# A two-layer macaron block in float32r: where the tiles of x and h begin in the SBUF

## The chip, the cores and the metric

The kernel runs on one core of one Trainium2 chip. Its time is the device time in microseconds (us) of one execution, and lower is better. Three executions of the kernel before were timed; their median is what a version is judged by.

## The reference

The input is x of 512 tokens by 1024 features, in float32. Two layers follow one another, each in the same frame:

```
mod = silu(c) @ ada_w[i] + ada_b[i]          # 9 vectors of 1024: shift, scale, gate, three times
h = rms_norm(x) * (1 + sc1) + sh1;  x += 0.5 * g1 * swiglu(h, wg1, wu1, wd1)   # hidden 2816
h = rms_norm(x) * (1 + sc2) + sh2;  x += g2 * mix(h)
h = rms_norm(x) * (1 + sc3) + sh3;  x += 0.5 * g3 * swiglu(h, wg2, wu2, wd2)
x = rms_norm(x)
```

In layer 0 `mix` is differential attention (8 heads, two softmaxes of 64-wide queries and keys per head, values 128 wide, a bias by distance, causal). In layer 1 it is a spatial gating unit: gelu(h @ w_in) split into u and v, v normed and mixed over each 128 tokens by a lower-triangular matrix per group, times u, times w_out. Nearly all arithmetic is in the products with the weights: gate, up and down of four feed-forward blocks, and the projections of the two mixers.

## The kernel before

Features lie on partitions. x is eight tiles x0 to x7 of 128 features by 512 tokens (2048 bytes on each partition). The normed input h is held in two parts, hh (h rounded to float32r) and hl (the rest), eight tiles each, of the same shape. A weight chunk arrives by DMA in a raw tile wr, and `Stream.conv` (line 183) splits it into wh and wl in the same manner: a cast on ACT, a subtraction on DVE. `Stream.get` keeps the loads some chunks ahead of the products. Every product is then three matmuls, `mm3` (line 582): wh with the high part of the activation, wh with the low part, wl with the high part. Each matmul has its own load of the stationary operand.

Four shapes of these products carry the kernel:

- Gate and up of the feed-forward blocks (`ffn`, line 702) and the u half of the gating unit: stationary is a 128x128 piece of wh or wl, moving is hh or hl with all 512 tokens. The rows call them mm<-hh,wh, mm<-hl,wh and mm<-hh,wl, moving operand first.
- Down (`down_g`, line 637): stationary is again a piece of wh or wl, moving is an activation pair from the pool `apool` (named a). The last half of a block's columns is done in two halves of 256 tokens, so that the next norm can begin.
- The first group of gate and up of the later feed-forward blocks goes by halves of 256 tokens too, moving hh and hl.
- `tm_block` (line 602), for q, k, v of the attention and the v half of the gating unit: stationary is a 128-token piece of hh or hl, moving is wh or wl with 256 columns (mm<-wh,hh, mm<-wh,hl, mm<-wl,hh).

The scheduler of the tile framework orders the instructions of each engine by priority and adds the waits; only at the start (lines 380 to 880, up to the end of `start_products`) are they issued as written. Pools take their room in the SBUF in the order in which they are opened (lines 78 to 84), one after the other, and tiles within a pool likewise, each rounded up to 32 bytes per partition. The first pool, `cst`, holds ident (512 bytes), mhalf (128), ones (4, so 32), ones_r (512), then the 24 tiles of x, hh and hl, then some thirty small vectors.

What this makes of the addresses can be worked out from the sizes: ident begins at 16512 bytes, which is 128 beyond a multiple of 512 (class 128). ones_r begins at 17184, class 288. x0 begins at 17696, class 288, and since each of the 24 tiles is 2048 bytes, all of x, hh and hl are of class 288. The small vectors behind them bring `cst` to 68928, class 320; there wrp begins, and all tiles of wrp, whp, apool, npool and accp and the large ones of the pools opened later (the feed-forward's, the attention's) are multiples of 512 bytes or follow such, so wr, wh, wl, a, acc, silu, qk, v and qkT are all of class 320. Class 288 is 32 beyond a multiple of 64; class 320 is a multiple of 64.

Of the kernel before, what the change touches and what calls it, by code (L numbers as in the profile page):

```python
# [11 lines left out]
F32 = mybir.dt.float32  # L12
# [7 lines left out]
P = 128  # L20
S = 512
# [15 lines left out]
def _bucket_runs():  # L37
    """Runs of equal bucket along y, where the distance is n = S - 1 - y."""
    n = np.arange(S - 1, -1, -1)
    nf = np.maximum(n, 1).astype(np.float32)  # L40
    large = MAX_EXACT + (
        np.log(nf / MAX_EXACT) / math.log(MAX_DIST / MAX_EXACT) * (BUCKETS - MAX_EXACT)
    ).astype(np.int32)
    b = np.where(n < MAX_EXACT, n, np.minimum(large, BUCKETS - 1))
    runs, lo = [], 0
    for y in range(1, S + 1):
        if y == S or b[y] != b[lo]:
            runs.append((lo, y, int(b[lo])))
            lo = y
    return runs  # L50


class InOrder:
    """An engine; while on, its instructions are issued in the order they are written."""

# [14 lines left out]
def macaron_kernel(ctx: ExitStack, tc: tile.TileContext, T: dict, out: bass.AP):  # L70
# [6 lines left out]

    cst = ctx.enter_context(tc.tile_pool(name="cst", bufs=1))
    wrp = ctx.enter_context(tc.tile_pool(name="wrp", bufs=4))
    whp = ctx.enter_context(tc.tile_pool(name="whp", bufs=5))  # L80
    apool = ctx.enter_context(tc.tile_pool(name="apool", bufs=24))
    npool = ctx.enter_context(tc.tile_pool(name="npool", bufs=2))
    tiny = ctx.enter_context(tc.tile_pool(name="tiny", bufs=4))
    accp = ctx.enter_context(tc.tile_pool(name="accp", bufs=1))
# [31 lines left out]
    def rsqrt(v, n):  # L116
        """v [P, n] positive and normal -> 1/sqrt(v): bit estimate, then Newton steps."""
        if n <= 4:
            y = tiny.tile([P, 32], F32, tag="rq_y", name=nm("rq_y"))
            G.tensor_tensor(out=y[:, :n], in0=v, in1=mhalf[:, :n], op=ALU.pow)  # L120
            return y[:, :n]
        i = tiny.tile([P, 32], U32, tag="rq_i", name=nm("rq_i"), bufs=2)
        j = tiny.tile([P, 32], I32, tag="rq_j", name=nm("rq_j"), bufs=2)
        ts(i[:, :n], v.bitcast(U32), 1, ALU.logical_shift_right)
        ts(j[:, :n], i[:, :n].bitcast(I32), -1.0, ALU.mult, 1597463007.0, ALU.add)
        y = j[:, :n].bitcast(F32)
        for it in range(3):
            t = tiny.tile([P, 32], F32, tag="rq_t", name=nm("rq_t"), bufs=2)
            tt(t[:, :n], y, y, ALU.mult)
            u = tiny.tile([P, 32], F32, tag="rq_u", name=nm("rq_u"), bufs=2)  # L130
            stt(u[:, :n], t[:, :n], -0.5, v, ALU.mult, ALU.mult)
            z = tiny.tile([P, 32], F32, tag="rq_y", name=nm("rq_y"))
            stt(z[:, :n], u[:, :n], 1.5, y, ALU.add, ALU.mult)
            y = z[:, :n]
        return y

    # ---------------------------------------------------------------- constants
    ident = cst.tile([P, P], F32, name="ident")
# [11 lines left out]

    x = [cst.tile([P, S], F32, name=f"x{d}") for d in range(KT)]
    h_hi = [cst.tile([P, S], F32R, name=f"hh{d}") for d in range(KT)]
    h_lo = [cst.tile([P, S], F32R, name=f"hl{d}") for d in range(KT)]

    ada_w, ada_b = T["ada_w"], T["ada_b"]

    # ------------------------------------------------------------- weight stream
    plan = []
# [53 lines left out]

    # ------------------------------------------------------- modulation vectors
    mod = {}
    acc_of = {}

    def finish_mod(l, m, ps):
        """ps [P, KT] holds c_act @ ada_w for this vector, one column per feature tile."""
        o = cst.tile([P, KT], F32, name=f"mod{l}_{m}")
# [30 lines left out]
    def flush_late(force=False):  # L250
        """The sums over partitions follow once the accumulation is surely through."""
        for it in list(late):
# [19 lines left out]

    # --------------------------------------------------------------------- plan
    ffn_w = {
# [6 lines left out]
    def groups_of(first):  # L281
        """FFN hidden tiles: two halves, each a list of groups of tiles."""
        if first:
            h1 = [[0, 1, 2]] + [[f, f + 1] for f in range(3, 11, 2)] + [[11]]
            h2 = [[f, f + 1] for f in range(12, 22, 2)]
        else:
            h1 = [[f, f + 1] for f in range(0, 12, 2)]
            h2 = [[f, f + 1] for f in range(12, 22, 2)]
        return h1, h2
# [8 lines left out]
    def get_k(key, nk):  # L298
        """The chunks of one block of columns, as they come: (k0, kn, hi, lo)."""
        for k0, kn in kchunks(nk):  # L300
# [77 lines left out]

    # ------------------------------------------------------------ start: loading
    in_order(True, V, A, PE, G, SY)  # L380
# [48 lines left out]
    def small_inputs():  # L429
        """Gains and biases of the rest, a column per tile of 128 features."""  # L430
        rows = a_tile()
# [27 lines left out]
    def attn_inputs():  # L459
        """The bias by distance for every head, and lambda."""  # L460
        # tab[h, y] = 8 * bias at distance S-1-y, masked beyond
        rb = a_tile()[:H, :BUCKETS]
# [9 lines left out]
        nc.gpsimd.dma_start(out=sc[:, S:], in_=tail[:H, : NCOL - S])  # L472
        # bias[h, p, c] = tab[h, 127 - p + c]: distance p + 384 - c
        par["bias"] = dram.tile([H, P, S], F32, name="bias")
# [11 lines left out]

    # ------------------------------------------------------------------- norms
    def bcast_tokens(r, tts, dst):
        """dst[:, 128*i ...] = r[token] on every partition."""
        for i, t in enumerate(tts):  # L490
# [8 lines left out]
    class Norm:  # L499
        """RMS norm over features (partitions and tiles) of x, by halves of the tokens."""  # L500

# [23 lines left out]
        def s1(self, hf):  # L525
# [9 lines left out]
            if self.pre is not None:  # L535
                # of the scaled x / sqrt(v): 1 / (sqrt(v) sqrt(m / v + EPS)) = 1 / sqrt(m + EPS v)
                m = tiny.tile([P, 2], F32, tag="nw", name=nm("nw"))
# [44 lines left out]
    def mm3(ps, w_hi, w_lo, a_hi, a_lo, first, last):  # L582
        """ps += w.T @ a with the operands split in two parts each."""
        PE.matmul(ps, lhsT=w_hi, rhs=a_hi, start=first, stop=False)
        PE.matmul(ps, lhsT=w_hi, rhs=a_lo, start=False, stop=False)
        PE.matmul(ps, lhsT=w_lo, rhs=a_hi, start=False, stop=last)

    # ------------------------------------------------------------------ phases
    def glu(pg, pu, fp):
# [5 lines left out]
    def split(v):  # L595
        """v = hi + lo, hi its rounding to float32r and lo the rest."""
        hi, lo = a_tile(F32R), a_tile(F32R)
# [13 lines left out]
    def token_major(key, done):  # L611
        """h (tokens) x one block of 256 columns; done(half, bank) takes two token tiles each."""
        W = list(get_k(key, KT))
# [8 lines left out]
    def token_major2(keys, dones):  # L622
        """Two blocks at once, the first half of the tokens ahead of the second."""
        Ws = [list(get_k(key, KT)) for key in keys]
# [12 lines left out]
    def down_g(tag, acts, gate, norm=None):  # L637
        """x += gate * (w.T @ acts); with norm, its sums and first half follow, the rest is pending."""
        na = len(acts)
# [112 lines left out]

    # --------------------------------------------------- start: x, norm, first mods
    sp2 = tiny.tile([P, 2, NB], F32, tag="ss0", name="sp2")
# [129 lines left out]

    # ------------------------------------------------------- differential attention
    with tc.tile_pool(name="attn", bufs=2) as at:
# [9 lines left out]
        def proj(p):  # L896
            """Generator: the products of a pair of heads, q and k normed and turned."""
            res = R[p] = {}
# [61 lines left out]
        def stage_a(n):  # L960
            """Logits, bias and softmax of one tile of queries of one head."""
            p, hh, i = steps[n]
# [30 lines left out]
        def stage_b(n):  # L993
            """The attention matrix turned, keys on partitions."""
            p, hh, i = steps[n]
# [8 lines left out]
        def stage_c(n):  # L1004
            """Times the values; after a head's (for the last one: half a head's) last tile its norm."""
            p, hh, i = steps[n]
# [24 lines left out]
        def stage_d(p, hh, t0, nt):  # L1031
            """A head's output turned, features on partitions."""
            o = oo.pop((p, hh, t0))
# [65 lines left out]

    # ------------------------------------------------------------- spatial gating  # L1100
    with tc.tile_pool(name="sgu", bufs=1) as sg:
# [73 lines left out]

    # -------------------------------------------------------------------- output
    oa = out.rearrange("o s d -> (o s) d")
# [50 lines left out]
```

## Time and profile before

| | us |
|---|---|
| three timed executions | 1961.03, 1957.12, 1956.90 (median 1957.12) |
| the profiled execution, first to last instruction (its span, the one time that the profile gives) | 1959.7 |
| TensorE (PE) busy in it | 1929.9 (98%) |
| VectorE (DVE) busy | 1081.5 (55%) |
| ScalarE (ACT) busy | 684.0 (35%) |
| GpSimd (POOL) busy | 69.8 (4%) |

PEld is TensorE's load of stationary operands, which runs beside PE. A matmul's row gives its own duration, some 0.4 us for 512 columns; successive ones overlap, so the time from one start to the next is shorter, and it is read from a stretch of the chain of waits: length over count. Nearly all instructions are issued by a helper, so their line is L63, and groups are told apart by tile names.

### The profile page before, as it was taken

What the parts mean: (1) busy time and instruction counts of PE and PEld (TensorE: products, weight loads), DVE (VectorE), ACT (ScalarE), POOL (GpSimd) and SP (SyncE); (2) the same over time, 40 slices, a digit from 0 to 9 for tenths busy, and PEclk for the clock granted to TensorE, in tenths of its full rate; (3) what the DMA queues carried; (4) which work ended last, traced back from release to release, by engine and by line L of the source; (5) the groups of instructions that cost most, each with busy time, mean ns of one, the idle gap of its engine ahead of it and who ended that gap; (6) DMA issues with size and microseconds to landing.
All of it is one profiled execution on the core that took longest, in us unless ns stands there. A gap on an engine that the chain in (4) does not pass through costs nothing.

```text
span 1959.7 us, 25722 instructions
## 1 busy us (share of the span) xinstructions
PE 1929.9 (98%) x10263; PEld 1635.1 (83%) x10263; DVE 1081.5 (55%) x1953; ACT 684.0 (35%) x1095; POOL 69.8 (4%) x81
## 2 busy tenths in 40 slices
PE   7999999999999999999999999999999999999998
PEld 6788888899997888888889888888898898888888
DVE  6856465576778854444457644444577763333332
ACT  5433123235555542222334232223252342222223
POOL 4300000000000000000000000000000000000000
PEclk8899999999999999999999999999999999999999
DMA  9666565532222254444443544443544333333321
GB/s 264 202 190 201 152 205 162 183 124 87 76 76 78 65 179 124 138 135 143 121 148 98 162 127 141 139 140 100 169 134 156 98 98 97 97 97 94 89 86 44
DMA packets 204109, 255.74 MB, mean 130 GB/s; under 512 B 9167, under 2 KB 177265, under 8 KB 203989
## 3 DMA queue, kind: packets, MB, share of 16 engines
q1 hardware_dynamic: 201552, 249.60, 41.6%
q0 software_dynamic: 2336, 4.46, 0.8%
q8 instruction: 80, 1.31, 0.3%
q14 instruction: 41, 0.33, 0.0%
q10 hardware_dynamic: 100, 0.04, 0.0%
HBM read 251.94 MB, written 4.21 MB: 131 GB/s over the span
## 4 chain that ended last, share of the span: by engine, by line
PE 93%; DVE 4%; ACT 1%; SPq 1%; DMA 1%; issue 0%; POOL 0%; POOLq 0%; ACTq 0%; DVEq 0%
PE mm L63 91%; PE sm L63 2%; DVE acc L63 2%; DVE a L63 1%; SPq L63 1%; DVE wl L63 0%; ACT a L63 0%; POOL rq_y L63 0%; DMA ada<-in_ada_w_dram 0%; ACT wh L63 0%; DVE x L63 0%; DVE hl L63 0%; DMA a<-in_x_dram 0%; ACT sq L63 0%; DVE A L63 0%
## 5 line engine op out<-in xcount | busy, mean ns | idle before, releaser
L63 DVE TENSOR_TENSOR wl<-wr,wh 128x1024 fp32r<-128x1024 f32 (+1 forms) x320 | 384.3, 1203 | 421.1 <-ACT wh L63 418.3
L63 PE MATMUL mm<-hh,wh 128*128 128x512 f32 (+1 forms) x1568 | 602.9, 385 | 8.3 <-ACT hh L63 8.3
L63 PE MATMUL mm<-hl,wh 128*128 128x512 f32 (+1 forms) x1568 | 602.4, 384 | 1.7 <-DVE hl L63 1.7
L63 PE MATMUL mm<-hh,wl 128*128 128x512 f32 (+1 forms) x1568 | 600.9, 384 | 0.0
L63 ACT CAST wh<-wr 128x1024 fp32r<-128x1024 f32 (+2 forms) x328 | 336.7, 1029 | 743.4 <-PE mm L63 680.9
L63 PE MATMUL mm<-a,wh 128*128 128x512 f32 (+1 forms) x2112 | 542.0, 346 | 0.0
L63 PEld LDWEIGHTS mm<-a,wh 128*128 128x128 f32 x2112 | 368.7, 190 | 50.9 <-DVE mx L63 1.3
L63 PE MATMUL mm<-a,wl 128*128 128x512 f32 (+1 forms) x1056 | 364.5, 345 | 2.2 <-DVE wl L63 2.2
L63 PEld LDWEIGHTS mm<-hh,wh 128*128 128x128 f32 x1568 | 296.9, 189 | 72.6 <-ACT hh L63 10.5
L63 PEld LDWEIGHTS mm<-hl,wh 128*128 128x128 f32 x1568 | 297.1, 189 | 65.8 <-DVE hl L63 3.6
L63 PEld LDWEIGHTS mm<-hh,wl 128*128 128x128 f32 x1568 | 296.6, 189 | 62.9 <-DVE wl L63 0.2
L63 DVE SCALAR_TENSOR_TENSOR acc<-wr,c_col,acc 128x1024 f32<-128x1024 f32 x112 | 143.7, 1283 | 185.8 <-DMA wr<-in_ada_w_dram 185.4
L63 PEld LDWEIGHTS mm<-a,wl 128*128 128x128 f32 x1056 | 200.8, 190 | 26.6 <-DVE wl L63 2.9
L63 PE MATMUL mm<-wh,hh 128*128 128x256 f32 x512 | 146.5, 287 | 0.0
L63 PE MATMUL mm<-wl,hh 128*128 128x256 f32 x512 | 142.9, 280 | 0.0
L63 PE MATMUL mm<-wh,hl 128*128 128x256 f32 x512 | 142.6, 280 | 0.0
L63 ACT CAST a<-silu 128x512 fp32r<-128x512 f32 x88 | 54.6, 621 | 152.1 <-DVE silu L63 152.1
L63 PEld LDWEIGHTS mm<-wh,hh 128*128 128x128 f32 x512 | 96.4, 188 | 8.6 <-issue 6.9
L63 DVE SCALAR_TENSOR_TENSOR x<-mm,mod,x 128x512 f32<-128x512 f32 (+1 forms) x116 | 70.7, 619 | 59.4 <-PE mm L63 58.9
L63 PEld LDWEIGHTS mm<-wl,hh 128*128 128x128 f32 x512 | 96.4, 188 | 0.0
L63 PEld LDWEIGHTS mm<-wh,hl 128*128 128x128 f32 x512 | 96.1, 188 | 0.1
L63 DVE TENSOR_TENSOR silu<-silu,mm 128x512 f32<-128x512 f32 x88 | 60.1, 686 | 44.0 <-PE mm L63 43.8
(166 smaller groups left out, 1149.6 us busy)
## 6 DMA issues: line engine op xcount, KB each, us to landing
wr<-in_ada_w_dram SPq DMA_DIRECT2D x128, 512.0 KB, 3.6
wr<-in_ffn_wg_dram SPq DMA_DIRECT2D x84, 512.0 KB, 3.9
wr<-in_ffn_wu_dram SPq DMA_DIRECT2D x84, 512.0 KB, 3.9
wr<-in_ffn_wd_dram SPq DMA_DIRECT2D x84, 512.0 KB, 3.5
wr<-in_attn_w_qkv_dram SPq DMA_DIRECT2D x24, 512.0 KB, 3.6
ada<-in_ada_w_dram SPq DMA_DIRECT2D x16, 512.0 KB, 6.0
wr<-in_sgu_w_in_dram SPq DMA_DIRECT2D x16, 512.0 KB, 3.8
wr<-in_attn_w_o_dram SPq DMA_DIRECT2D x8, 512.0 KB, 3.5
```

The source lines that it names most:

```text
L63: r = f(*a, **kw)
```

## The change

Two pools change places and one is new. `tiny`, the pool of small vectors (5632 bytes, eleven times 512), is opened second instead of sixth, and x, hh and hl move from `cst` into a pool of their own, `hxp`, opened third. `cst` then ends at 19776 (class 320), `tiny` at 25408 (class 320), and there x0 begins; the 24 tiles of x, hh and hl are of class 320 like all other large tiles. wrp begins at 74560 and whp, apool and npool move up with it by 5632 bytes, which leaves their class at 320; accp and what is opened later stays where it was. ident and ones_r stay at classes 128 and 288. No instruction is added or taken out, and none has another shape or operand. The diff also empties docstrings and comment lines, which issue nothing.

```
     cst = ctx.enter_context(tc.tile_pool(name="cst", bufs=1))
+    tiny = ctx.enter_context(tc.tile_pool(name="tiny", bufs=4))
+    hxp = ctx.enter_context(tc.tile_pool(name="hxp", bufs=1))
     wrp = ctx.enter_context(tc.tile_pool(name="wrp", bufs=4))
     whp = ctx.enter_context(tc.tile_pool(name="whp", bufs=5))
     apool = ctx.enter_context(tc.tile_pool(name="apool", bufs=24))
     npool = ctx.enter_context(tc.tile_pool(name="npool", bufs=2))
-    tiny = ctx.enter_context(tc.tile_pool(name="tiny", bufs=4))
     accp = ctx.enter_context(tc.tile_pool(name="accp", bufs=1))
...
-    x = [cst.tile([P, S], F32, name=f"x{d}") for d in range(KT)]
-    h_hi = [cst.tile([P, S], F32R, name=f"hh{d}") for d in range(KT)]
-    h_lo = [cst.tile([P, S], F32R, name=f"hl{d}") for d in range(KT)]
+    x = [hxp.tile([P, S], F32, name=f"x{d}") for d in range(KT)]
+    h_hi = [hxp.tile([P, S], F32R, name=f"hh{d}") for d in range(KT)]
+    h_lo = [hxp.tile([P, S], F32R, name=f"hl{d}") for d in range(KT)]
```

## Rows read from the trace of the kernel before

**Rows 1.** The page: busy time of the engines, and the granted clock in 40 slices.
```profile
PE 1929.9 (98%) x10263; PEld 1635.1 (83%) x10263; DVE 1081.5 (55%) x1953; ACT 684.0 (35%) x1095; POOL 69.8 (4%) x81
...
PEclk8899999999999999999999999999999999999999
```

**Rows 2.** Stretches of the run: length, busy time and count of PE, granted clock, DMA share, GB/s.
```profile
690.00:1040.00 350.00, 350.00 (x1639) 1.00 0.44 136
1480.00:1880.00 400.00, 399.56 (x1952) 1.00 0.33 101
```

**Rows 3.** The page, chain of waits: shares of the span by engine.
```profile
PE 93%; DVE 4%; ACT 1%; SPq 1%; DMA 1%; issue 0%; POOL 0%; POOLq 0%; ACTq 0%; DVEq 0%
```

**Rows 4.** PE's waits: releaser, us in total, times, longest us.
```profile
PE mm L63 <- ACT hh L63: 8.3, 5, 3.0
PE mm L63 <- DVE wl L63: 2.2, 3, 1.5
```

**Rows 5.** Groups of matmuls by shape: count, busy us, mean ns, idle before.
```profile
L63 PE MATMUL mm<-hh,wh 128*128 128x512 f32 x1376 | 549.1, 399 | 8.3 <-ACT hh L63 8.3
L63 PE MATMUL mm<-a,wh 128*128 128x512 f32 x1216 | 376.7, 391 | 0.0
L63 PE MATMUL mm<-a,wh 128*128 128x256 f32 x896 | 165.3, 286 | 0.0
L63 PE MATMUL mm<-wh,hh 128*128 128x256 f32 x512 | 146.5, 287 | 0.0
L63 PE MATMUL mm<-hh,wh 128*128 128x256 f32 x192 | 53.8, 283 | 0.0
```

**Rows 6.** Chain of waits in gate and up, moving hh and hl: start, length, count.
```profile
1079.93 80.27 PE mm L63 x344
```
**Rows 7.** Chain of waits in down, 512 columns, moving a.
```profile
1194.94 60.07 PE mm L63 x265
1714.88 50.32 PE mm L63 x222
```
**Rows 8.** Chain, 256 columns: moving a; moving wh, stationary hh; moving hh, stationary wh.
```profile
1920.00 16.44 PE mm L63 x137
...
1439.89 28.36 PE mm L63 x243
...
1588.00 12.07 PE mm L63 x102
```
**Rows 9.** Chain within down: four matmuls of 512 columns, moving a, stationary ones_r.
```profile
387.42 0.93 PE sm L63 x4
```
**Rows 10.** Chain within attention: eight transposes of 128 columns, each with its own load.
```profile
515.00 0.87 PE sm L63 x8
```
**Rows 11.** Groups on DVE and ACT that touch x or h, and their like on a.
```profile
L63 DVE SCALAR_TENSOR_TENSOR x<-mm,mod,x 128x512 f32<-128x512 f32 x60 | 44.3, 748 | 29.1 <-PE mm L63 28.9
L63 DVE SCALAR_TENSOR_TENSOR a<-a,rs,a 128x512 f32<-128x512 f32 x8 | 6.0, 750 | 0.2
L63 ACT ACTIVATE sq<-x 128x512 f32<-128x512 f32 x15 | 9.3, 628 | 10.9 <-DVE x L63 9.6 <-DVE ssq L63 1.1
L63 ACT ACTIVATE a<-a 128x512 f32<-128x512 f32 x15 | 9.4, 632 | 13.0 <-DVE a L63 11.2 <-DMA a<-in_x_dram 1.8
```
**Rows 12.** Chain at the start: one of six such pieces of DVE, and PE behind them.
```profile
52.85 4.59 DVE acc L63 x6
...
69.14 32.92 PE mm L63 x129
```
## The prediction

> **What bounds the kernel now.** I read four views, from coarse to fine. The page first: PE is busy for 98% of the span, no other engine for more than 55%, and the clock is granted in full in all but the first two of 40 slices [rows 1]. The stretches next: from 690 to 1040 us PE is busy for 350.00 of 350.00 us, from 1480 to 1880 for 399.56 of 400, with the DMA engines below a half [rows 2]. The chain of waits puts 93% of the span on PE [rows 3], and PE's own waits are a few us: the longest groups are 8.3 us for hh and 2.2 us for wl [rows 4]. So in the feed-forward blocks PE never runs dry, and what counts there is not who waits but how far apart the starts of successive matmuls are. For that I divide pieces of the chain by their counts.
>
> The reader should see that the same instruction has two paces. In gate and up, moving hh or hl, 344 matmuls take 80.27 us: 233.3 ns each [rows 6]. In down, moving a, 265 take 60.07 us and 222 take 50.32 us: 226.7 ns each in both pieces [rows 7]. Both kinds have 512 columns, a stationary 128x128 piece of wh or wl loaded for each, a full clock and no wait. Their own durations differ in the same sense, 399 against 391 ns [rows 5]. What differs is the moving operand: hh and hl begin at class 288, a at class 320 like the stationary. [...]
>
> One more place bears on it: four matmuls in the midst of a down stretch move a (class 320) with ones_r (class 288) as stationary, and take 0.93 us, 232.5 ns each [rows 9]. So the slow pace appears too when the moving operand is of class 320 and only the stationary is of class 288. Whether the cause is that the two classes differ, or that either one is off a multiple of 64, the change removes it, since after it both operands of every weight product are of class 320.
>
> At 256 columns the order is the other way round. Moving a against wh, both 320: 137 in 16.44 us, 120.0 ns. Moving wh against hh, so 320 and 288: 243 in 28.36 us, 116.7 ns. Moving hh against wh: 102 in 12.07 us, 118.3 ns [rows 8]. There, equal classes are the slower ones, by 2 to 3 ns.
>
> **The change part by part.** No instruction is added, removed or reshaped, and no wait or queue is new. What moves is where operands lie, so the sum is counts times differences of pace.
>
> *Gate, up and the u half of the gating unit, 512 columns.* There are three groups of 1376, of which one stands in [rows 5]: 4128 matmuls. 144 of them belong to the start (8 feature tiles, 6 banks, 3 each), which DVE paces: six pieces of six accumulations of some 4.6 us each stand in the chain up to 67 us, and PE follows behind, 129 matmuls in 32.92 us, 255 ns each, part of it at the lower clock [rows 12]. I count nothing for them; if the last 129 gained in full, that would be 0.9 us more. The other 3984 run in stretches like that of [rows 6], and I let them go from 233.3 to the pace of [rows 7]: 3984 x 6.66 ns = 26.5 us less. All of it lies on the chain. Bounds: nothing, if they stay at 233.3. [...]
>
> *Products with h as stationary, 256 columns.* Three groups of 512, one of them in [rows 5]: 1536 matmuls, which go from classes 320 and 288 to 320 and 320. The nearest row with these is the 120.0 ns of moving a. 1536 x 3.3 ns = 5.1 us more. Most of them lie in the attention, where PE is the engine that the chain runs through, so I take the price in full. Bounds: at 116.7 nothing is lost; the quickest full-width step with a load of its own is 8 transposes in 0.87 us, 109 ns [rows 10], which would give 11.8 us back.
>
> *First group of gate and up, by halves, 256 columns.* Three groups of 192, one in [rows 5]: 576 matmuls, 118.3 to 120.0: 576 x 1.7 ns = 1.0 us more. Bounds: nothing, and 5.4 us less at 109 ns.
>
> *DVE and ACT.* x is read and written by DVE, h written by ACT and DVE. On tiles of class 288 they cost what they cost on class 320: 748 ns against 750 for a three-operand DVE instruction, 628 against 632 for a square on ACT [rows 11]. I cost them at nothing, and a few ns either way would be hidden under PE. Small vectors move as well, but to where no large operand's class changes. No DMA writes x, hh or hl, so the DMAs see the same classes as before.
>
> *What is late next.* PE would ask for weight chunks 3% sooner in gate and up. DMA is at 0.33 to 0.44 of its time there [rows 2], DVE at 55% over the run [rows 1]; neither becomes the bound. If that cover failed, PE's 2.2 us of waits on wl [rows 4] would grow, and I allow 1 us in the range.
>
> Sum: -26.5 + 5.1 + 1.0 = -20.4 us. Against the profiled execution's span of 1959.7 us this is 1939.3. That span lies 2.6 us over the median of the three executions, within their spread; taken off the median, 1957.1 - 20.4 = **1936.7 us**.
>
> [...]
>
> **The rivals.**
>
> *The wide ones gain, the narrow ones lose nothing.* The 120.0 ns of the narrow matmuls in down may come from their moving operand, half tiles of a, rather than from equal classes. Then the result is -26.5 alone, 1930.6 us, or 1929.6 if the start gains its 0.9 too. For it: the only row with equal classes at 256 columns is of one kind. Against it: three kinds with three pairs of classes have three paces, each steady.
>
> *The gain is there only in part.* The pace could settle at neither of the two where streams alternate, since the matmuls of [rows 9] run at 232.5 amid a 226.7 stretch. Half of the 26.5 us, with the narrow ones' price: -13.2 + 6.1 = -7.1, 1950 us.
>
> *No change.* The slow pace belongs to the stage or to the region in the SBUF (x, hh, hl and ones_r all lie below all weight tiles, and still do after the change), not to the class. For it: [rows 9] has ones_r in that region as well. [...] Time: 1957.1.
>
> *Slower.* Equal classes are what costs: moving and stationary operands that begin in one class meet in the SBUF, and this decides where the load of the stationary operand takes up most of the matmul's time, that is at 256 columns; the wide pace stays, as under the case before. Then 5.1 + 1.0 us are added: 1963.2 us. For it: the 120.0 against 116.7 and 118.3 ns. Against it: at 512 columns equal classes are the fast ones, and the wide ones hold most of the time.
>
> **How the numbers follow.** Forecast 0.56; wide gain without the narrow loss 0.21; in part 0.06; no change 0.12; slower 0.05. Three executions of this kernel lie within 0.2% (3.9 us) of one another but for one, so I call 0.2% what can be told from no change. The first three cases are all beyond it: faster 0.83; within it 0.12; slower 0.05, since 6.1 us is 0.3%. The range runs from 1927, the second case less a spread of 2 to 3 us between executions, to 1951, the case in part with 1 us for late chunks: it holds 0.83 and leaves out the last two cases.
>
> **What would show it.** In the profile after, the chain's piece in gate and up should have 226.7 ns per matmul in place of 233.3, and the mean duration of mm<-hh,wh at 512 columns should go from 399 to some 391 ns. The pieces with wh moving should go to 120 ns; if they stay at 117, the second case holds. Down should keep its 226.7. The pieces with ones_r, whose class stays 288, should keep 232. DVE and ACT groups on x and h should not move by more than a few ns. The prediction is wrong if gate and up still stand at 233, or if PE's waits in the feed-forward blocks grow from a few us to more than ten.

## The result and the profile after

The changed kernel takes 1935.95 us (median of four executions, 1935.40 to 1940.03); the kernel before, with one more execution beside it, 1958.58 us (1956.90 to 1961.03). The ratio is 0.989 with a 95% interval of 0.9876 to 0.9904, so 19 to 24 us less. The forecast was 1936.7 us. The profiled execution after took 1940.03 us, the longest of its four, as the profiled one before (1961.03 us) was of its own; it spans 1938.3 us, 21.4 us less than the span before.

The page after, busy times: the number of instructions is the same, and PE alone is busy for less, 1906.1 us in place of 1929.9.

```profile
PE 1906.1 (98%) x10263; PEld 1637.2 (84%) x10263; DVE 1080.6 (56%) x1953; ACT 684.3 (35%) x1095; POOL 69.8 (4%) x81
```

The chain of waits after (start, length, count), in gate and up, in down, with wh and wl moving against h, in the first group of gate and up by halves, in the halves of down, and at the matmuls with ones_r:

```profile
1079.85 60.29 PE mm L63 x266
...
1189.83 50.32 PE mm L63 x222
...
1424.96 25.07 PE mm L63 x209
...
1572.33 10.79 PE mm L63 x90
...
1904.95 9.12 PE mm L63 x76
...
380.73 0.93 PE sm L63 x4
```

Divide each length by its count. Gate and up: 226.7 ns, where [rows 6] had 233.3. Down: 226.7 ns, as in [rows 7]. The three narrow kinds: 120.0, 119.9 and 120.0 ns, where [rows 8] had 116.7, 118.3 and 120.0. With ones_r: 232.5 ns, as in [rows 9]; its class stayed at 288. The groups by shape agree with [rows 5] and [rows 11]: the wide matmul of hh went from 399 to 392 ns, DVE's update of x stayed (748 to 747).

```profile
L63 PE MATMUL mm<-hh,wh 128*128 128x512 f32 x1376 | 539.7, 392 | 8.5 <-ACT hh L63 8.5
L63 PE MATMUL mm<-a,wh 128*128 128x512 f32 x1216 | 376.1, 390 | 0.0
L63 DVE SCALAR_TENSOR_TENSOR x<-mm,mod,x 128x512 f32<-128x512 f32 x60 | 44.3, 747 | 28.6 <-PE mm L63 28.5
```

Where the 21.4 us went can be read by stages: a stage runs from the start of its first matmul to the start of the first one of the next stage, read from the two traces; the differences are taken before rounding.

| stages | before, us | after, us | difference |
|---|---|---|---|
| up to the first product | 19.5 | 18.9 | -0.7 |
| gate and up (eight halves of blocks) and u of the gating unit | 1078.8 | 1053.3 | -25.5 |
| attention, with q, k, v | 188.3 | 190.8 | +2.5 |
| v of the gating unit | 48.3 | 49.3 | +1.0 |
| down, last projections, the end | 624.7 | 626.1 | +1.3 |

### The profile page after: what moved, and what is told of

It is laid out like the page before. It is cut to its first block, busy times and chain, and to the rows that moved or that the text cites. A ratio compares the mean times of both kernels' runs of the same rounds, so it can differ in the third digit from the quotient of the medians.

```text
span 1938.3 us, 25722 instructions
## 1 busy us (share of the span) xinstructions
PE 1906.1 (98%) x10263; PEld 1637.2 (84%) x10263; DVE 1080.6 (56%) x1953; ACT 684.3 (35%) x1095; POOL 69.8 (4%) x81
## 4 chain that ended last, share of the span: by engine, by line
PE 91%; DVE 5%; DMA 1%; ACT 1%; SPq 1%; issue 1%; POOL 0%; POOLq 0%; ACTq 0%; DVEq 0%
PE mm L63 89%; PE sm L63 2%; DVE acc L63 2%; DMA wr<-in_ada_w_dram 1%; DVE wl L63 1%; DVE a L63 1%; SPq L63 1%; ACT a L63 0%; ACT wh L63 0%; POOL rq_y L63 0%; DMA ada<-in_ada_w_dram 0%; DVE x L63 0%; DVE hl L63 0%; ACT sq L63 0%; DVE A L63 0%
## 5 line engine op out<-in xcount | busy, mean ns | idle before, releaser
L63 PE MATMUL mm<-hh,wh 128*128 128x512 f32 (+1 forms) x1568 | 593.8, 379 | 8.5 <-ACT hh L63 8.5
L63 PE MATMUL mm<-hl,wh 128*128 128x512 f32 (+1 forms) x1568 | 592.8, 378 | 1.4 <-DVE hl L63 1.4
L63 PE MATMUL mm<-hh,wl 128*128 128x512 f32 (+1 forms) x1568 | 591.2, 378 | 0.0
```

Source lines behind the costliest of these rows:

```text
L63: r = f(*a, **kw)
```

## The experiments

Two readings fitted the forecast equally well, and both compete with "region", the third case to be tested (x, hh and hl lie in another part of the SBUF): that a matmul is quick when both operands begin at multiples of 64 bytes (**multiple of 64**), and that it is quick when both begin at the same place modulo some size (**one class**, later **difference**). In what follows the difference is the start of the moving operand minus that of the stationary one. All runs give paces from the chain as above; their interval is that of the ratio to the kernel before.

**h off the class again, in its new place.**

```
+    pad1 = ctx.enter_context(tc.tile_pool(name="pad1", bufs=1))
+    pad1.tile([P, 8], F32, name="pad1_t")
     hxp = ctx.enter_context(tc.tile_pool(name="hxp", bufs=1))
+    pad2 = ctx.enter_context(tc.tile_pool(name="pad2", bufs=1))
+    pad2.tile([P, 120], F32, name="pad2_t")
```

pad1 takes 32 bytes of each partition, pad2 480.

> The changed kernel with 32 bytes left free ahead of x, hh and hl and 480 behind them: these 24 tiles begin at class 352 (32 beyond a multiple of 64), all other large tiles stay at 320, and the pool order and the region are those of the changed kernel. Theory 'classes' (the pace of a matmul follows from where its two operands begin, and 320 against 320 is quick at 512 columns): gate and up go back to about 233.3 ns per matmul, the products with h stationary to about 117 ns, and the time to about 1936 + 21 = 1957 us. Rival 'region' (x, hh and hl are quick because of the place behind the small vectors, or the new pool): gate and up stay at 226.7 ns, the time at 1936 us.

Measured: 1959.79 us, ratio 1.0014 (1.0003 to 1.0025). The chain in gate and up:

```profile
1079.96 80.27 PE mm L63 x344
```

That is 233.3 ns again. Same pool, same order, same region, 32 bytes further: all of the gain is gone. "Region" falls. The narrow ones with wh moving average 118.3 ns, not 117, which is 2 us of the time above the expected 1957.

**h 64 beyond the weights.** The same edit with 64 bytes ahead and 448 behind.

> The changed kernel with 64 bytes left free ahead of x, hh and hl and 448 behind: class 384, a multiple of 64, but not the class of the weights (320). Theory A 'multiple of 64' (a matmul of 512 columns is quick when both operands begin at multiples of 64): gate and up stay at 226.7 ns, h stationary at 120 ns, time 1936 us. Theory B 'one class' (it is quick when both begin at the same place modulo 512): gate and up go back to about 233 ns, h stationary to about 117, time 1957 us. If wide ones are quick and narrow ones too, 226.7 and 117, the time is about 1936 - 4 = 1932 us.

Measured: 1945.61 us (1940.93 to 1946.70), ratio 0.9931 (0.9917 to 0.9946). Three pieces of its chain, two in gate and up and one with wh moving:

```profile
889.90 50.13 PE mm L63 x219
...
1279.86 50.17 PE mm L63 x215
...
1429.90 23.14 PE mm L63 x202
```

The same code runs at 228.9 ns from 890 us and at 233.4 ns from 1280 us, each steady over tens of us, and which of the two a block gets differs. Neither is 226.7, though both operands are multiples of 64: that theory falls for the wide ones. The narrow ones run at 114.6 ns, quicker than in either kernel so far.

**All large tiles at class 352.** The 32 bytes ahead of hxp, nothing behind it.

> The changed kernel with 32 bytes left free ahead of x, hh and hl and nothing taken back: all large tiles, h, x, weights and activations, begin at class 352, so still one class, but 32 beyond a multiple of 64. Theory B 'one class': paces as in the changed kernel, 226.7 ns at 512 and 120 at 256 columns, time 1936 us. Theory A 'multiple of 64': gate and up at 233.3 ns or more, and down with 512 columns (1824 matmuls) as well; 26.5 + 12.1 us more, less up to 10 us if the narrow ones go to 117 ns: some 1965 to 1975 us.

Measured: 1936.69 us, ratio 0.9892 (0.9877 to 0.9906). Chain in gate and up, and in down:

```profile
1079.93 60.29 PE mm L63 x266
...
1194.91 35.13 PE mm L63 x155
```

Both at 226.7 ns, with every operand 32 off a multiple of 64. "Multiple of 64" is refuted a second time; "one class" holds.

**h 256 away from the weights.** 256 bytes ahead and 256 behind.

> The changed kernel with 256 bytes left free ahead of x, hh and hl and 256 behind: class 64, a multiple of 64, half of 512 away from the weights' class. Theory A 'multiple of 64': gate and up at 226.7 ns, h stationary at 120 ns, 1936 us. Theory B 'one class': gate and up about 233 ns, 1957 us. If the distance of the two operands matters in steps of its own, the pace differs from that with class 384.

Measured: 1937.22 us, ratio 0.9889 (0.9872 to 0.9905). Chain in gate and up, and with wh moving:

```profile
1079.96 60.07 PE mm L63 x265
...
1425.00 25.08 PE mm L63 x209
```

226.7 and 120.0 ns. By the letter this agrees with "multiple of 64" and contradicts "one class modulo 512"; together with the two runs before, it leaves a class modulo 256 or a part of it.

**128 beyond.** 128 bytes ahead and 384 behind.

> The changed kernel with x, hh and hl at class 448, 128 beyond the class of the weights (320). So far a difference of 0 or 256 between the two operands gave 226.7 ns at 512 and 120 ns at 256 columns, a difference of 32 either way 233.3 and some 117 to 118, a difference of 64 between 228.9 and 233.3, and 114. Theory 'period 128': 128 is like 0, paces 226.7 and 120, time 1936 us. Theory 'period 256': 128 is a difference of its own, with gate and up away from 226.7 ns and h stationary away from 120 ns; time anywhere from 1930 to 1957 us.

Measured: 1959.47 us, ratio 1.0011 (1.0002 to 1.0021), and the chain in gate and up:

```profile
1089.78 60.44 PE mm L63 x259
```

That is 233.4 ns. A period of 128 falls, and 256 is left.

**64 before, and 192 beyond.** 448 ahead and 64 behind; 192 ahead and 320 behind.

> The changed kernel with x, hh and hl at class 256, 64 before the class of the weights. If only the size of the difference counts, it goes as with 64 beyond: gate and up at 228.9 or 233.3 ns by stretches, h stationary at 114 ns, 1941 to 1947 us. If the side counts (which operand runs ahead of the other), gate and up lock to one pace in all stretches: 228.9 ns would give 1936 + 8.8 - 12.7 = 1932 us, 233.3 ns some 1950 us.

> The changed kernel with x, hh and hl at class 0, 192 beyond the class of the weights. Theory 'period 128': like a difference of 64, gate and up at 228.9 or 233.3 ns, h stationary at 114 ns, 1941 to 1947 us. Theory 'period 256': like 64 before (class 256), whatever that gives.

Measured: 1958.68 us, ratio 1.0005 (0.9994 to 1.0015), and 1957.91 us, ratio 1.0004 (0.9994 to 1.0014). In both, gate and up lock to 233.3 ns in all stretches, which the first expectation priced at 1950 us; it took too much for the narrow ones: at 114 ns for all of them the sum is 1950, with the paces that they took it is some 1955, and the rest I have not taken apart. Of h at class 256, the chain in gate and up, with wh moving, and with hh moving by halves:

```profile
1089.80 60.43 PE mm L63 x259
...
1439.97 28.50 PE mm L63 x242
...
1587.83 10.22 PE mm L63 x90
```

233.3, 117.8 and 113.6 ns. So the side counts. In the run with h at 384 the narrow ones with wh moving had a difference of -64, that is 192, and 114.6 ns; here it is those with hh moving that have 192, and they take 113.6, while those with wh moving have 64 and take 117.8. With h at class 0 the difference for wh moving is 64 again (modulo 256), and the chain there gives 117.8 ns, beside 233.3 in gate and up:

```profile
1089.81 60.20 PE mm L63 x258
...
1439.98 23.79 PE mm L63 x202
```

A period of 256 fits all of these.

**The weights moved, not h.** In the kernel before, 480 bytes left free ahead of wrp and 32 behind whp, so that the weights join h at class 288.

> The kernel before with the weight tiles wr, wh and wl moved to class 288 by 480 bytes left free ahead of them and 32 behind; x, hh and hl stay at 288, where they were, and a, acc and all else at 320. Theory 'difference' (the pace follows from the difference of the two operands' classes): gate and up go to 226.7 ns without h being moved at all, h stationary to 120 ns, but down, whose operands now differ by 32, goes from 226.7 to 233.3 ns at 512 columns (1824 matmuls, 12.1 us more) and from 120 to some 117 at 256 (1344 matmuls, 4 us less): about 1936 + 12 - 4 = 1944 us. Rival 'h itself' (what counted was that h was off a multiple of 64, or its region): gate and up stay at 233.3 ns, time 1957 us or above.

Measured: 1943.94 us, ratio 0.9927 (0.9912 to 0.9942), as expected. Chain in gate and up, in down, and in the halves of down:

```profile
1079.81 60.29 PE mm L63 x266
...
1189.91 40.13 PE mm L63 x172
...
1909.93 8.24 PE mm L63 x70
```

Gate and up are at 226.7 ns with h untouched; down has gone from 226.7 to 233.3 and its halves from 120 to 117.7. The pace belongs to the pair of operands.

**A curve in one run.** The tiles of wh and wl are made 256 bytes longer, and the split weights go some bytes into them, another number for each group (`shift_of` takes the next of a list for each new group; the list and its body are left out here):

```
+    SH = [0, 4, 8, 16, 32, 48, 64, ...]
+    def shift_of(key):
...
-            hi = whp.tile([P, 1024], F32R, tag="wh", name=nm("wh"))
+            hi = whp.tile([P, 1088], F32R, tag="wh", name=nm("wh"))[:, shift_of(it["key"]) // 4 :]
```

> The changed kernel with the tiles of wh and wl 256 bytes longer and the split weights put 0 to 240 bytes into them, another shift for each group of gate and up (0, 4, 8, 16, 32, 48 and so on to 240) and each block of q, k, v and of the gating unit's v (0, 16, 32 to 240); some buffers of small vectors are fewer, to make room. One run then holds a curve: the pace against the difference (moving minus stationary, modulo 256). Theory 'difference modulo 256' expects what the other runs gave wherever the same difference comes up: at 512 columns 226.7 ns at 0, 233.3 at 32, 128, 192 and 224, 228.9 or 233.3 at 64; at 256 columns 120 at 0, 117 at 32, 117.7 at 64, 119 at 128, 113.7 at 192, 118.3 at 224. Rival 'which tile it is': a shift within the tile changes nothing, all groups at 226.7 and 120 ns. Open: whether any difference beats 226.7 ns at 512 columns, and what 4, 8 and 16 bytes do. Time somewhere between 1936 and 1960 us.

Measured: 1948.81 us in one execution. Pieces of its chain within the groups of the last feed-forward block whose difference is 32, 16, 0, 252, 248 and 208:

```profile
1594.90 18.20 PE mm L63 x78
...
1616.83 19.27 PE mm L63 x85
...
1637.90 19.27 PE mm L63 x85
...
1660.85 18.35 PE mm L63 x79
...
1682.90 18.22 PE mm L63 x79
...
1813.81 19.37 PE mm L63 x83
```

The paces are 233.3, 226.7, 226.7, 232.3, 230.6 and 233.4 ns. Over the run, as means of the distances between starts (those over 300 ns at 512 columns and over 180 ns at 256 left out, and the first 90 us too):

| difference | 0 | 16 | 32 | 48 | 64 | 80 | 96 | 112 | 128 | 144 | 160 | 176 | 192 | 208 | 224 | 240 | 248 | 252 |
|---|---|---|---|---|---|---|---|---|---|---|---|---|---|---|---|---|---|---|
| 512 columns, h moving, ns | 226.9 | 227.7 | 233.3 | 232.4 | 233.4 | 230.1 | 233.4 | 233.3 | 232.9 | 233.3 | 234.2 | 232.0 | 233.3 | 233.3 | 233.3 | 231.1 | 230.7 | 232.3 |
| 256 columns, h stationary, ns | 120.3 | 118.3 | 116.9 | 118.4 | 117.8 | 119.9 | 119.8 | 114.8 | 118.6 | 118.2 | 118.3 | 119.1 | 117.3 | 117.9 | 118.4 | 117.3 | - | - |

A narrow number comes from one block of 96 matmuls. Two pairs of blocks alternate in the run (0 with 16, 192 with 208) and are told apart by the order in the program.

No difference beats 0 for the wide ones; 16 comes close, while 4 or 8 bytes the other way (252, 248) already cost most. At 240 one group ran at 226.8 and two at 233.3. For the narrow ones 0 is the slowest, by little ahead of 80 and 96. Two points are not as expected: the narrow block at 192 has 117.3 ns where earlier runs had 113.6 and 114.6, and all wide groups at 64 have the slower of their two paces. "Which tile it is" falls: the shift within the tile does what moving the tile did.

**A version that takes both.** The shift follows the use of a chunk: none for 512 columns, a difference of 192 for 256.

```
+    def shift_of(key):
+        if key[0] in ("q", "k", "v", "sv"):
+            return 192
+        if key[0] in ("g", "u") and key[3] == 0 or key[0] == ("o", 1) or "f" in key:
+            return 64
+        return 0
```

> The changed kernel with the tiles of wh and wl 256 bytes longer, and the split weights put into them at a shift that follows what the chunk is used for: none where the matmuls have 512 columns, and where they have 256 a shift that makes moving minus stationary 192 modulo 256 (192 bytes for q, k, v and the gating unit's v, 64 bytes for the halves of down, the last projection of the attention and the first groups of gate and up). Some buffers of small vectors are fewer, to make room. Theory 'difference modulo 256': the wide ones keep 226.7 ns, the narrow ones go from 120 to about 113.7 ns: 1344 in down and 576 in gate and up gain 6.3 ns each, 12.1 us; the 1536 of q, k, v gained 6 us over the run when h was at class 384; 1936 - 18 = 1918 us. If the narrow ones are not on the path, or lock to 117 to 118 ns, 1925 to 1932 us. Rival 'which tile it is': no change from 1936 us.

Measured: 1923.37 us (1922.78 to 1924.89), ratio 0.9822 (0.9808 to 0.9835): quicker than both kernels. Chain in gate and up, with wh moving, and in the halves of down:

```profile
1069.84 60.29 PE mm L63 x266
...
1414.96 25.13 PE mm L63 x220
...
1894.90 5.65 PE mm L63 x48
```

226.7, 114.2 and 117.7 ns. The halves of down and the first groups lock to the slower of two narrow paces for much of the time (means of 116.9 and 117.2 ns over the run, where 113.7 was expected; over their 1920 matmuls that is 6 us), so 1918 was missed by 5 us.

**Another difference for the narrow ones.** `return 112` and `return 144` in place of 192 and 64.

> As the run that shifts the split weights for matmuls of 256 columns, with another shift: moving minus stationary 112 modulo 256 in place of 192 (112 bytes for q, k, v and the gating unit's v, 144 bytes for the halves of down, the last projection of the attention and the first groups of gate and up). With 192 the three kinds ran at 116.9, 117.3 and 114.8 ns, between a pace of 113 to 114 and one of 118. In the scan 112 gave 114.7 ns in its one block of v. If 112 holds 114 ns in all: 1344 x 2.9 + 576 x 3.3 = 5.8 us less than 1923.4, 1917.6 us. If it also changes between two paces, 1921 to 1926 us.

Measured: 1927.68 us, ratio 0.9849 (0.9835 to 0.9862), above both expectations. Chain with wh moving, and in the halves of down:

```profile
1419.95 20.10 PE mm L63 x176
...
1894.91 8.16 PE mm L63 x68
```

114.2 and 120.0 ns: the same difference gives two paces. (The scan's block at 112 was one of k, with h stationary, so nothing had shown the other two kinds at 112.) With h stationary 112 is as good as 192; with a or hh moving it is as slow as 0. So at 256 columns the difference alone does not settle the pace.

**No shift, all else of that version.** Both returns at 0.

> The same kernel with no shift at all: the longer tiles of wh and wl and the fewer buffers of small vectors are there, but the split weights begin at the head of their tiles, and moving minus stationary is 0 everywhere. If the gain from 1936 to 1923 us came from the shift, this is back at the changed kernel's 1936 us with 120 ns at 256 columns. If it came from what was done to make room (buffers, where tiles lie), this stays at 1923 us.

Measured: 1933.08 us, ratio 0.9875 (0.9862 to 0.9889). The chain with wh moving:

```profile
1419.98 20.04 PE mm L63 x167
```

That is 120.0 ns, as in the changed kernel. The shifts are worth 9.7 us (1933.1 to 1923.4) by the medians and 10.4 by the ratios; the two profiled executions differ by 7.6 in their spans, of which the stages with h stationary hold 5.4. The other 2.9 us between the changed kernel and this run are not shown to be anything: the intervals of the two ratios, 0.9876 to 0.9904 and 0.9862 to 0.9889, overlap.

## Why the prediction was right

- *The bound.* The chain in the feed-forward blocks was PE's own pace, and a pace that fell by 2.9% shortened the stages by what it said. PE's waits for wl are 2.9 us after, 2.2 before [rows 4].
- *The size.* Forecast -20.4 us; measured -22.6 by the medians (19 to 24), -21.4 between the profiled executions. That 1936.7 came within 1 us of the measured 1935.95 is in part luck: the base of the sum, 1957.1, became 1958.58 with one more execution. (The span of 1959.7 us belongs to the execution of 1961.03, so that one lay 3.9 us over the median and not 2.6.)
- *Gate, up and u.* Forecast -26.5, and +1.0 for the first groups by halves, which lie in the same stages: -25.5. Measured: -25.5. The step that carried the sum was right in its count, its pace and its place on the path. Behind the first block it is so without luck: 3552 x 6.66 ns less the 1.0 is -22.7, measured -22.8. In the first block two things that the sum leaves out cancel. The start's 144 matmuls took 1.6 us less. Through it PE waits again and again for hh, up to 3.0 us at a time before and after, with DVE's accumulations in the chain [rows 12], and in both traces the granted clock falls to 0.50 for a few us: before, from 70 to 74 us, where DVE paces it no longer, and after, from 48 to 52 us, where DVE still does; from 70 to 74 us it is 1.00 there. And some products with ones_r at the end of the block came some 1.6 us late, behind ACT and DVE. Their group had no idle time before; after, it has this:

```profile
L63 PE MATMUL sm<-a,ones_r 128*128 128x512 f32 x64 | 21.0, 409 | 1.2 <-ACT a L63 1.0 <-DVE a L63 0.2
```

  With h at class 64 that group has 0.0 us of idle time, and in the runs with all tiles at 352 and without shifts it has none either, so this wait comes and goes.
- *h stationary.* Forecast +5.1, measured +3.5 (2.5 in the attention, 1.0 in the gating unit). The pace went to 120.0 as said. The term took [rows 8]'s 116.7 ns, from the gating unit, for the attention as well, and took the price in full there. In the attention the distances between starts average 117.1 ns before and 119.8 after, 2.7 and not 3.3, and it is no pure stream of these matmuls: 1152 x 3.3 ns = 3.8 us showed as 2.5.
- *Not counted.* 1.7 us more in the down ahead of the gating unit: the chain after has a DMA there that lands late.

```profile
1374.42 5.85 DMA wr<-in_ada_w_dram
```

  The same stage takes 60.7 us in the run with all tiles at 352 and 60.5 in the one without shifts, against 63.4 before and 65.0 after, so this is a wait that comes and goes between executions and no cost of the classes. It is the late chunk for which the range kept 1 us.
- *The rival without the narrow loss* is refuted: all three narrow kinds stand at 120 ns. (Its second time is 1929.7 by its own terms, not 1929.6.) *In part* is refuted for this change; a pace that locks to either of two values does exist, at other differences (h at 384: 228.9 and 233.4 ns). *No change* fell with the result, and its reason, the region, with the runs that move h by 32 bytes within one region and the weights instead of h. *Slower* named a true price, equal classes at 256 columns (120.0 ns against 116.7 and 118.3), and missed that the wide matmuls gain some six times as much (26 us against 4.4). Its reason, that the two operands meet, was a guess: the loads take 188 ns beside matmuls of 287 at 256 columns and 189 beside 399 at 512 in the trace before, but no run shows a meeting.
- *Multiples of 64.* That either operand is off a multiple of 64, one of the two causes that [rows 9] left open, is not what made the pace slow: with all operands at class 352 it is 226.7 ns. The forecast did not depend on it, since under both readings the change puts both operands at 320.

## What to carry to other kernels

In a stream of matmuls that each load their own stationary operand, look at the distance between starts, not at busy time: PE was 98% busy at both paces. If the same shape has two paces in two stages, compare where moving and stationary operands begin, modulo 256 bytes, the period that fits the runs here (226.7 ns at differences of 0 and 256, 233.4 at 128). Here, in float32r with 128x128 stationary pieces, matmuls of 512 columns were quickest when both begin at the same place (226.7 ns, against 233.3 at most other differences), and matmuls of 256 columns slowest (120 ns, against 113.6 at best); which other place is best for those has to be tried for each kind. A few bytes of padding set it (32 bytes took gate and up from 226.7 to 233.3 ns), and an offset within a longer tile sets it per use (offsets of 192 and 64 bytes were worth 9.7 us).

## What the runs showed of the hardware that was not expected

- In these runs the pace of a wide matmul went with the difference of the two operands' starts modulo 256: 226.7 ns at 0 (class 320 against 320, 352 against 352, 288 against 288, 64 against 320), 227.7 at 16, 233.3 to 233.4 at 32, 128, 192 and 224. Why the pace depends on it is not shown by any run here.
- At some differences a stream has two steady paces and keeps the one that it falls into: 228.9 and 233.4 ns in blocks of one execution at a difference of 64, 226.8 and 233.3 at 240.
- At 256 columns the order turns: 120 ns at 0, and 113.6 to 120.0 elsewhere. Beyond equal classes, shifts per use were worth some 10 us (1933.1 to 1923.4). What decides between 114 and 118 ns, and why a difference of 112 gives 114.2 ns in one kind and 120.0 in another, stays open.
